# A two-layer streaming encoder step: low halves of the moving operands at multiples of 256 bytes, shared mixer tiles, the residual through another queue

## The chip, the cores and the metric

The kernel runs on one core of one Trainium2 chip. The metric is device time in microseconds of one execution, as the median of several runs; the kernel before took 2676.73 us (three runs, 2674.0 to 2679.26). Profiles come from one further execution of the same program.

## The reference

One inference step for two request groups that share weights: 256 frames of a new stream and 32 next frames of a running one, 288 columns together. Layer 0 is a mixer of retention and gated linear attention (GLA) heads, then a convolutional feed-forward network (FFN); layer 1 is chunked band attention, then an FFN. All is float32, with a model width of 2048.

```
def trunk(x, pos, ret_in, gla_in, k_in, v_in, conv_in, p):
    for l in range(DEPTH):
        h = rmsnorm(x, p['norm_mix_g'][l])
        if l % 2 == 0:
            mix, s_r, s_g = ab_mixer(h, pos, ...)
        else:
            mix, nk, nv = c_mixer(h, ...)
        x = x + mix
        h = rmsnorm(x, p['norm_ffn_g'][l])
        f, buf = conv_ffn(h, ...)
        x = x + f
    y = rmsnorm(x, p['norm_final_g'])

def conv_ffn(h, conv_buf, w_up, conv_w, conv_b, w_down):
    up = jnp.einsum('btd,df->btf', h, w_up)
    g, u = jnp.split(up, 2, axis=-1)
    ...
    act = jax.nn.silu(gc) * u
    return jnp.einsum('btf,fd->btd', act, w_down), gp[:, -(CONV_W - 1):]
```

The outputs are the 288 frames, the new retention and GLA states, the new attention rows and the last rows of the convolutions.

## The kernel before

Activations lie transposed in SBUF: 128 features on the partitions, the 288 frames along them. Every weight matrix is cut into tiles of 128 by 128, and one `project` (L65) makes 128 output features: for each of 16 (or 22) input tiles k it adds products into one PSUM tile of 288 columns, called acc.

A float32 product is made of three faster ones. `weights` (L54) loads a chunk of eight weight tiles (512 KB, through SP's queue, into one of four buffers w), rounds it on ACT into a high part wh (L61, type fp32r) and takes the rest on DVE as a low part wl (L62), three buffers each. The activations are split in the same way, on ACT and DVE, into a high and a low tile. `passes` (L81) then issues three matmuls:

```
        nc.tensor.matmul(ps, lhsT=h, rhs=xh, start=first, stop=False)
        nc.tensor.matmul(ps, lhsT=h, rhs=xl, start=False, stop=False)
        nc.tensor.matmul(ps, lhsT=l, rhs=xh, start=False, stop=last)
```

They are L83, L84 and L85. The weight is the stationary operand, the activation the moving one: 288 columns, 1152 bytes on each partition. L83 and L85 stream the high tile, L84 the low one. The moving operands are named x0 to x15 (the normalised input of a projection; a profile's row says x), and b (16 pairs in one tile: the outputs of the mixers, the input of the output projections and of the FFN's down projection, whose 6 further pairs are b16 to b21 in a pool of the FFN). In each of them the low half stands right behind the high half of the same k.

The stages in order: the first products (L87), where the input x_first comes in ten pieces, each with the residual, two weight columns and a small part of a third for one or two k, and is split as it arrives; the GLA heads and retention heads (`ab_mixer`, L467), whose small full-precision matmuls stand between the projections; the output projection (`out_proj`, L277), which adds each result to the residual x (DVE, L284), squares and splits it for the next norm (ACT L170, DVE L171); the FFN (L288); the attention heads; a second output projection; the second FFN, with the final norm.

The residual x of the first layer is overwritten by squares during the mixer, so it is read again from memory before the output projection (L220, four DMAs of four k each on SP). Its SBUF room is that of the mixer's pool, so the reload waits until the mixer's last users of that room are done, among them the DMAs that write the retention states out (L808).

A tile framework orders the instructions of each engine when the program is built, and gives each a wait for what it needs. An engine and a DMA queue work in order: what stands behind a waiting instruction waits too. SP issues weights and little else; POOL issues the small loads and the outputs and does small copies.

Of the kernel before, what the change touches and what calls it, by code (L numbers as in the profile page):

```python
# [5 lines left out]
F32 = mybir.dt.float32  # L6
F32R = mybir.dt.float32r
# [5 lines left out]
P = 128  # L13
D = 2048
KD = D // P
TP = 256
TS = 32
T = TP + TS
FF = 5632
NF = FF // P  # L20
HALF = NF // 2
# [4 lines left out]
RANK = 16  # L26
# [5 lines left out]
GRP = P // TS  # L32
# [5 lines left out]
class Trunk:  # L38
# [48 lines left out]
    def first_products(self, src, xw, lo_h):  # L87


        nc = self.nc  # L90
        ps = [self.acc_ps.tile([P, 512], F32, name="acc", tag="acc")[:, :T] for _ in range(N_FIRST + 1)]
        cuts = (0, 1, 2, 3, 4, 6, 8, 10, 12, 14, 16)

        for _ in range(8):
            nc.tensor.matmul(self.mm()[:, :P], lhsT=self.ones, rhs=self.ones, start=True, stop=True)
        for c, (i, j) in enumerate(zip(cuts, cuts[1:])):
            n = j - i
            nc.sync.dma_start(xw[:, i:j, :], src[:, i:j, :])
            w = xw[:, i:j, T : T + N_FIRST * P].rearrange("p k (o m) -> p k o m", o=N_FIRST)
            wlo = xw[:, i:j, T + N_FIRST * P :]  # L100
            lo = lo_h[:, i:j, :]
            tile = lambda tag: self.wp.tile([P, WCH, P], F32R, name=tag, tag=tag, bufs=3)[
                :, : N_FIRST * n, :
            ].rearrange("p (k o) m -> p k o m", o=N_FIRST)
            h, l = tile("wh"), tile("wl")
            for k in range(i, j):
                self.gain_in(k, 0)
                if k == i:
                    if c:
                        nc.scalar.copy(h, w)  # L110
                    else:
                        nc.vector.tensor_copy(h, w)
                    nc.vector.tensor_tensor(l, w, h.bitcast(F32), op=ALU.subtract)
                    nc.gpsimd.tensor_copy(lo[:, :, :RANK], wlo)
                    nc.gpsimd.tensor_tensor(
                        lo[:, :, RANK : 2 * RANK], wlo, lo[:, :, :RANK].bitcast(F32), op=ALU.subtract
                    )
                first, last = k == 0, k == KD - 1
                at = k - i
                for o in range(N_FIRST):  # L120
                    nc.tensor.matmul(ps[o], lhsT=h[:, at, o, :], rhs=self.xh[k], start=first, stop=False)
                for o in range(N_FIRST):
                    nc.tensor.matmul(ps[o], lhsT=h[:, at, o, :], rhs=self.xl[k], start=False, stop=False)
                for o in range(N_FIRST):
                    nc.tensor.matmul(ps[o], lhsT=l[:, at, o, :], rhs=self.xh[k], start=False, stop=last)
                nc.tensor.matmul(ps[-1], lhsT=lo[:, at, :], rhs=self.xh[k], start=first, stop=False)
                nc.tensor.matmul(ps[-1], lhsT=lo[:, at, :], rhs=self.xl[k], start=False, stop=last)
        return ps
# [67 lines left out]
    def run(self, ctx):  # L196
        nc, a = self.nc, self.a

        ones = self.const("ones", [P, P + 32])
        self.ones, self.eps = ones[:, :P], ones[:, P : P + 1]  # L200
        xs = [self.const(f"x{k}", [P, 2, T], F32R) for k in range(KD)]
        self.xh, self.xl = [[x[:, i, :] for x in xs] for i in range(2)]
        b_all = self.const("b", [P, KD, 2, T], F32R)
        self.bh_all, self.bl_all = b_all[:, :, 0, :], b_all[:, :, 1, :]
        self.bh, self.bl = [[b_all[:, k, i, :] for k in range(KD)] for i in range(2)]
        self.R = self.const("R", [P, T])
        nc.vector.memset(self.ones, 1.0)
        nc.vector.memset(self.eps, EPS)
        self.gains = self.const("gains", [P, 5, KD], F32, a["gains"], nc.scalar)
        self.sq_last = None  # L210
        with self.tc.tile_pool(name="in", bufs=1) as pool:
            sums = self.start(pool)
        with self.tc.tile_pool(name="ab", bufs=1) as pool:
            self.ab_mixer(pool, *sums)
        with self.tc.tile_pool(name="x", bufs=1) as xp:

            x = xp.tile([P, KD * T + 16], F32, name="x", tag="x")[:, : KD * T].rearrange("p (k t) -> p k t", t=T)
            self.x = [x[:, k, :] for k in range(KD)]
            for k in range(0, KD, 4):
                nc.sync.dma_start(x[:, k : k + 4, :], a["xT"][:, k : k + 4, :])  # L220
            self.out_proj(a["w_out_ab"], 1, (WCH, 0))
            with self.tc.tile_pool(name="f0", bufs=2) as pool:
                self.ffn(pool, 0, 2, x)
            with self.tc.tile_pool(name="c", bufs=2) as pool:
                self.chain(
                    self.att_heads(pool), 3,
                    lambda: self.out_start(a["w_out_att"], (0, WCH), 2),
                )
            self.out_proj(a["w_out_att"], 3, (0, WCH))
            with self.tc.tile_pool(name="f1", bufs=2) as pool:  # L230
                self.ffn(pool, 1, 4, x)
# [18 lines left out]
    def start(self, pool):  # L250

        nc, a = self.nc, self.a
        w = a["w_in"]

        nc.scalar.activation(self.R[:, :1], self.ones[:, :1], AF.Abs_reciprocal_sqrt)
        xw = self._one(pool, "xw", [P, KD, T + N_FIRST * P + RANK])
        x_in = xw[:, :, :T]
        self.x = [x_in[:, k, :] for k in range(KD)]


        lo_h = self._one(pool, "lo_h", [P, KD, P], None, F32R)
        nc.gpsimd.memset(lo_h.bitcast(F32)[:, :, 2 * RANK :], 0.0)
        k0, q0, lo_ps = self.first_products(a["x_first"], xw, lo_h)
        self.ident = self.const("ident", [P, P], F32, a["ident"], nc.sync)

        self.w2 = self.const("w2", [P, 512 + 224])[: 2 * RANK + 1, :512]
        nc.sync.dma_start(self.w2, a["w2"])
        v0 = self.input_product(w[VB])
        self.first_squares(x_in)

        self.norm_stat()
        v1 = self.mm()[:, :T]
        second = lambda part: self.project(w[VB + 1], self.xh, self.xl, KD, chunks=(0, WCH), part=part, ps=v1)
        second(0)
        return k0, q0, v0, lo_ps, second
# [11 lines left out]

    def ffn(self, pool, layer, n, x_all):  # L288
        nc, a = self.nc, self.a
        bs = [self._one(pool, f"b{k}", [P, 2, T], None, F32R) for k in range(KD, HALF)]  # L290
        bh, bl = [old + [b[:, i, :] for b in bs] for i, old in ((0, self.bh), (1, self.bl))]
        convp = self._one(pool, "convp", [P, NF, 4], a["convp"][:, layer])
        hist = self._one(pool, "hist", [P, NF, 2], a["hist"][:, layer])
# [6 lines left out]
        for half in range(2):  # L300
            for fl in range(HALF):
                f = half * HALF + fl
# [18 lines left out]
                v = pool.tile([P, T], F32, name="v", tag="v")  # L321
# [22 lines left out]
        cuts = (0, 1, 4, 8, 12, 16)  # L344
# [22 lines left out]
    def head_out(self, pool, o, gates, hd, g):  # L367

        nc = self.nc
        sq = pool.tile([P, TP], F32, name="hsq", tag="hsq", bufs=1)  # L370
        sq2 = pool.tile([P, TP], F32, name="hsq2", tag="hsq2", bufs=1)
        nc.scalar.activation(sq, o[0], AF.Square)
        nc.scalar.activation(sq2, o[1], AF.Square)
        nc.vector.tensor_tensor(sq, sq, sq2, op=ALU.add)
# [92 lines left out]
    def ab_mixer(self, pool, k0, q0, v0, lo_ps, second):  # L467
# [37 lines left out]

        def ret(hd):
            if hd == 0:
                late["cos"], late["sin"] = one("cosR", [P, T], a["cos"]), one("sinR", [P, T], a["sin"])
                for t in late.values():
                    nc.gpsimd.tensor_tensor(t, t, self.R, op=ALU.mult)  # L510
                late["kdec"] = one("kdec", [P, H_RET, 2], a["kdec"])
            aside = {0: gla_sample, H_RET - 1: ret_sample}.get(hd, iter(()))
            yield from self.ret_head(pool, hd, w, late["cos"], late["sin"], late["kdec"], hg, r4, rst, aside)
# [13 lines left out]
    def gla_head(self, pool, hd, w, sums, masks, eyem, hg, s4, sts, first):  # L527
# [11 lines left out]
        v.append(self.parted(pool, v1, "v1", s4["v"][:, 1, hd, :]))  # L539
        gate = lambda i: self.gate(pool, w[GB + 2 * hd + i], i, s4["z"][:, i, hd, :])  # L540
        z = [gate(0)] if first else []
        st = pool.tile([P, 256], F32, name="gst", tag="gst", bufs=GRP)
        nc.gpsimd.dma_start(st, a["state_gla"][hd])
        sts.append(st)

# [161 lines left out]
    def ret_head(self, pool, hd, w, cosR, sinR, kdec, hg, s4, sts, aside):  # L709
        nc, a = self.nc, self.a  # L710
        dec = pool.tile([P, 384], F32, name="dec", tag="dec")
        nc.gpsimd.dma_start(dec, a["dec"][hd])
        st = pool.tile([P, 2, 256], F32, name="rst", tag="rst", bufs=GRP)
        nc.gpsimd.dma_start(st, a["state_ret"][hd])
        sts.append(st.rearrange("p j v -> p (j v)"))

        def rope(base, name):
            z = [self.input_product(w[base + 2 * hd + i]) for i in range(2)]
# [177 lines left out]
    def att_sample(self, pool, g, kept, v4, bd):  # L896
# [13 lines left out]
        vt = pool.tile([P, P], F32, name="avt4", tag="avt4")  # L910
        nc.scalar.copy(vt, pv)
        s = pool.tile([P, T], F32, name="as4", tag="as4")
        own = pool.tile([P, GRP, TS], F32, name="own4", tag="own4")
        mx = pool.tile([P, 1], F32, name="mx4", tag="mx4")
        sm = pool.tile([P, 1], F32, name="sm4", tag="sm4")
        nc.vector.tensor_tensor(s, ps, bias, op=ALU.add)
# [20 lines left out]
        for i in range(2):  # L937
            for c, (_, _, vc) in zip(quarter, kept):
                nc.tensor.matmul(
                    po[c], lhsT=pT[:, 1 + i, c], rhs=vc[:, i, :], start=False, stop=i == 1, skip_group_check=True  # L940
                )
        o = pool.tile([P, P], F32, name="ao4", tag="ao4")
        nc.vector.tensor_scalar(o, po, sm, None, op0=ALU.mult)
        yield
        ps = self.mm()[:, :P]
# [139 lines left out]
```

## Time and profile before

| | |
|---|---|
| median of three runs | 2676.73 us (2674.0 to 2679.26) |
| the profiled execution | 2679.3 us, its span 2677.2 us |
| granted TensorE clock, mean | 0.998 |
| DMA | 448.27 MB, mean 167 GB/s |
| HBM | read 434.69 MB, written 10.40 MB |

The span runs from the first to the last instruction; the execution has 2.1 us around it. In a profile PE is the matmul engine and PEld its weight load; L83 is line 83 of the kernel. A group's row has its line, engine, operation, the tiles out<-in, the shape and the count; behind the bar the busy time in us and the mean length of one in ns, and then the idle time before it and who ended it. The rows of a timeline begin with the start and the length in us.

### The profile page before, as it was taken

To read this page: it belongs to the slowest core of one execution; us is meant where nothing else is said; L and a number is where in the kernel's file an instruction comes from. 1 tells how busy PE (TensorE), PEld (TensorE's weight loads), DVE (VectorE), ACT (ScalarE), POOL (GpSimd) and SP (SyncE) were. 2 spreads that over 40 slices of the span, in tenths; PEclk is the share of its full clock that TensorE was granted. 3 is DMA by queue.
4 is the path that set the end of the run, shared out by engine and by line. 5 is a ranking of instruction groups with operands and counts; after the bars stand their busy time and mean duration, and the time that the engine had idled before them with its cause. 6 is when DMAs were issued, how large, how long until landed. Compare 5 with 4: busy or idle time off the path is not lost. (4 is left out here: it accounts for less than half of the span.)

```text
span 2677.2 us, 48712 instructions
## 1 busy us (share of the span) xinstructions
PE 2661.0 (99%) x20079; PEld 2642.5 (99%) x20079; DVE 1560.8 (58%) x2593; ACT 1126.1 (42%) x1511; POOL 132.8 (5%) x459
## 2 busy tenths in 40 slices
PE   9999999999999999999999999999999999999998
PEld 9999999999999999999999999999999999999998
DVE  8665555566664456665555555556666545666544
ACT  7564445443333333334444443444333333333443
POOL 3000000000000000000021110000000000000000
PEclk9999999999999999999999999999999999999999
DMA  6444445555555555555565565555555555555554
GB/s 230 151 138 156 157 157 193 167 164 166 166 166 164 167 168 167 165 168 160 166 213 179 178 183 166 158 166 165 166 166 166 163 167 168 166 166 166 165 166 131
DMA packets 127227, 448.27 MB, mean 167 GB/s; under 512 B 16059, under 2 KB 16379, under 8 KB 127004
## 3 DMA queue, kind: packets, MB, share of 16 engines
q1 hardware_dynamic: 119852, 426.83, 51.5%
q0 software_dynamic: 7008, 18.29, 2.2%
q8 instruction: 157, 2.57, 0.4%
q14 instruction: 66, 0.54, 0.1%
q10 hardware_dynamic: 144, 0.04, 0.0%
HBM read 434.69 MB, written 10.40 MB: 166 GB/s over the span
## 5 line engine op out<-in xcount | busy, mean ns | idle before, releaser
L61 ACT CAST wh<-w 128x1024 fp32r<-128x1024 f32 (+1 forms) x812 | 839.2, 1034 | 1461.0 <-PE acc L84 1210.8
L62 DVE TENSOR_TENSOR wl<-w,wh 128x1024 fp32r<-128x1024 f32 (+1 forms) x812 | 976.4, 1203 | 738.4 <-ACT wh L61 737.4
L83 PE MATMUL acc<-x,wh 128*128 128x288 f32 x4432 | 1314.6, 297 | 0.0
L84 PE MATMUL acc<-x,wh 128*128 128x288 f32 x4432 | 1311.8, 296 | 0.0
L85 PE MATMUL acc<-x,wl 128*128 128x288 f32 x4432 | 1308.4, 295 | 0.0
L85 PEld LDWEIGHTS acc<-x,wl 128*128 128x128 f32 x4432 | 839.5, 189 | 0.3
L83 PEld LDWEIGHTS acc<-x,wh 128*128 128x128 f32 x4432 | 833.0, 188 | 1.6 <-issue 1.1
L84 PEld LDWEIGHTS acc<-x,wh 128*128 128x128 f32 x4432 | 833.3, 188 | 0.3
L83 PE MATMUL acc<-b,wh 128*128 128x288 f32 x1920 | 567.4, 296 | 0.5 <-ACT wh L61 0.5
L85 PE MATMUL acc<-b,wl 128*128 128x288 f32 x1920 | 566.2, 295 | 0.7 <-DVE wl L62 0.7
L84 PE MATMUL acc<-b,wh 128*128 128x288 f32 x1920 | 566.9, 295 | 0.0
L85 PEld LDWEIGHTS acc<-b,wl 128*128 128x128 f32 x1920 | 363.2, 189 | 1.2 <-DVE wl L62 1.0
L83 PEld LDWEIGHTS acc<-b,wh 128*128 128x128 f32 x1920 | 360.6, 188 | 1.3 <-ACT wh L61 1.1
L84 PEld LDWEIGHTS acc<-b,wh 128*128 128x128 f32 x1920 | 360.8, 188 | 0.1
L316 DVE SCALAR_TENSOR_TENSOR gc<-gp,convp,gc 128x290 f32<-128x290 f32 x176 | 91.2, 518 | 3.1
L322 DVE TENSOR_TENSOR v<-acc,R 128x288 f32<-128x288 f32 x88 | 40.3, 458 | 88.6 <-PE acc L85 88.6
L307 DVE TENSOR_TENSOR gp<-acc,R 128x256 f32<-128x256 f32 x88 | 37.4, 425 | 90.3 <-PE acc L85 90.1
L309 POOL COPY conv_out<-gp 128x2 f32<-128x2 f32 x88 | 16.4, 187 | 1309.3 <-DVE gp L307 1309.3
L147 ACT CAST b<-v 128x288 fp32r<-128x288 f32 x88 | 38.2, 434 | 16.1 <-DVE v L324 16.1
L323 DVE TENSOR_TENSOR v<-v,sg 128x256 f32<-128x256 f32 x88 | 37.4, 426 | 10.6 <-DVE v L322 1.8
L314 DVE TENSOR_SCALAR gc<-gp,convp 128x290 f32<-128x290 f32 x88 | 38.0, 431 | 9.4
L332 DVE TENSOR_TENSOR x<-x,acc 128x288 f32<-128x288 f32 x64 | 29.1, 454 | 19.2 <-PE acc L85 19.2
(301 smaller groups left out, 1140.1 us busy)
## 6 DMA issues: line engine op xcount, KB each, us to landing
w<-in_w_ffn_up SPq DMA_DIRECT2D x352, 512.0 KB, 3.7
w<-in_w_ffn_down SPq DMA_DIRECT2D x128, 512.0 KB, 3.7
w<-in_w_in SPq DMA_DIRECT2D x108, 512.0 KB, 3.8
w<-in_w_qkv SPq DMA_DIRECT2D x96, 512.0 KB, 3.8
w<-in_w_ffn_down SPq DMA_DIRECT2D x64, 384.0 KB, 3.2
w<-in_w_out_ab SPq DMA_DIRECT2D x32, 512.0 KB, 3.9
w<-in_w_out_att SPq DMA_DIRECT2D x32, 512.0 KB, 3.7
xw<-in_x_first SPq DMA_DIRECT2D x6, 560.0 KB, 7.9
```

Source lines behind the costliest of these rows:

```text
L61: nc.scalar.copy(h, w)
L62: nc.vector.tensor_tensor(l, w, h.bitcast(F32), op=ALU.subtract)
L83: nc.tensor.matmul(ps, lhsT=h, rhs=xh, start=first, stop=False)
L84: nc.tensor.matmul(ps, lhsT=h, rhs=xl, start=False, stop=False)
L85: nc.tensor.matmul(ps, lhsT=l, rhs=xh, start=False, stop=last)
L147: self.nc.scalar.copy(h, v)
L307: nc.vector.tensor_tensor(gp[:, 2 : TP + 2], g[:, :TP], self.R[:, :TP], op=ALU.mult)
L314: nc.vector.tensor_scalar(gc, gp[:, 0:W], cw[:, 0:1], cw[:, 3:4], op0=ALU.mult, op1=ALU.add)
L316: nc.vector.scalar_tensor_tensor(gc, gp[:, w : w + W], cw[:, w : w + 1], gc, op0=ALU.mult, op1=ALU.add)
L322: nc.vector.tensor_tensor(v, u, self.R, op=ALU.mult)
L323: nc.vector.tensor_tensor(v[:, :TP], v[:, :TP], s[:, :TP], op=ALU.mult)
L332: nc.vector.tensor_tensor(self.x[m], self.x[m], ps, op=ALU.add)
```

## The change

It has six parts. The first changes addresses, the others make room for it or move transfers.

1. x0 to x15, b and b16 to b21 get slots of 320 columns (1280 bytes) for each half in place of 288 (1152 bytes). The number of columns used stays 288.
2. The pad behind w2 shrinks from 224 to 32 columns.
3. The reload of the residual goes from SP's queue to POOL's, in eight DMAs of two k in place of four of four.
4. The GLA and retention states share one set of four tiles of 512 columns (st) where there were four of 256 (gst) and four of 512 (rst). Two GLA heads share a tile.
5. cos and sin take the two tiles of the softplus (sp); the second square of `head_out` takes a tile of the normed output (on); own4 and ao4 of the attention have one buffer in place of two.
6. The input pieces of the first products are single k up to k = 7 in place of k = 3.

The addresses in the built program, by their rest over 256 bytes:

| operand | before | after |
|---|---|---|
| high halves of x0 to x15, b, b16 to b21 | 0 | 0 |
| low halves of the same | 128 | 0 |
| weights w, wh, wl (each tile 512 bytes) | 64 | 64 |

```
+TB = 320
-        cuts = (0, 1, 2, 3, 4, 6, 8, 10, 12, 14, 16)
+        cuts = (0, 1, 2, 3, 4, 5, 6, 7, 8, 10, 12, 14, 16)
-        xs = [self.const(f"x{k}", [P, 2, T], F32R) for k in range(KD)]
+        xs = [self.const(f"x{k}", [P, 2, TB], F32R)[:, :, :T] for k in range(KD)]
-        b_all = self.const("b", [P, KD, 2, T], F32R)
+        b_all = self.const("b", [P, KD, 2, TB], F32R)[:, :, :, :T]
-            for k in range(0, KD, 4):
-                nc.sync.dma_start(x[:, k : k + 4, :], a["xT"][:, k : k + 4, :])
+            for k in range(0, KD, 2):
+                nc.gpsimd.dma_start(x[:, k : k + 2, :], a["xT"][:, k : k + 2, :])
-        self.w2 = self.const("w2", [P, 512 + 224])[: 2 * RANK + 1, :512]
+        self.w2 = self.const("w2", [P, 512 + 32])[: 2 * RANK + 1, :512]
-        bs = [self._one(pool, f"b{k}", [P, 2, T], None, F32R) for k in range(KD, HALF)]
+        bs = [self._one(pool, f"b{k}", [P, 2, TB], None, F32R)[:, :, :T] for k in range(KD, HALF)]
-        sq2 = pool.tile([P, TP], F32, name="hsq2", tag="hsq2", bufs=1)
+        sq2 = pool.tile([P, TP], F32, name="on", tag="on", bufs=2)
-                late["cos"], late["sin"] = one("cosR", [P, T], a["cos"]), one("sinR", [P, T], a["sin"])
-                for t in late.values():
+                late["cos"], late["sin"] = [pool.tile([P, T], F32, name="sp", tag="sp", bufs=2) for _ in range(2)]
+                for x, t in late.items():
+                    nc.gpsimd.dma_start(t, a[x])
                     nc.gpsimd.tensor_tensor(t, t, self.R, op=ALU.mult)
-        st = pool.tile([P, 256], F32, name="gst", tag="gst", bufs=GRP)
-        nc.gpsimd.dma_start(st, a["state_gla"][hd])
-        sts.append(st)
+        st = pool.tile([P, 512], F32, name="st", tag="st", bufs=GRP) if hd % 2 == 0 else None
+        sts += [st[:, :256], st[:, 256:]] if hd % 2 == 0 else []
+        nc.gpsimd.dma_start(sts[hd], a["state_gla"][hd])
-        st = pool.tile([P, 2, 256], F32, name="rst", tag="rst", bufs=GRP)
-        nc.gpsimd.dma_start(st, a["state_ret"][hd])
-        sts.append(st.rearrange("p j v -> p (j v)"))
+        st = pool.tile([P, 512], F32, name="st", tag="st", bufs=GRP)
+        nc.gpsimd.dma_start(st.rearrange("p (j v) -> p j v", j=2), a["state_ret"][hd])
+        sts.append(st)
-        own = pool.tile([P, GRP, TS], F32, name="own4", tag="own4")
+        own = pool.tile([P, GRP, TS], F32, name="own4", tag="own4", bufs=1)
-        o = pool.tile([P, P], F32, name="ao4", tag="ao4")
+        o = pool.tile([P, P], F32, name="ao4", tag="ao4", bufs=1)
```

From the diff's first line on, lines of the changed kernel stand one or two further down: the three passes are L84, L85 and L86 there.

SP's queue from the last weights of the mixer to the first of the FFN, before (w is a chunk of weights, in_ names its source, x the residual):

```order
L60 DMA w<-in_w_in 128x1024 x108
L60 DMA w<-in_w_out_ab 128x1024 x10
L220 DMA x<-in_xT 128x1152 x4
L60 DMA w<-in_w_out_ab 128x1024 x22
L60 DMA w<-in_w_ffn_up 128x1024 x88
```

and POOL's queue after the change, from the last outputs of the retention heads (so and st are state tiles, dec a decay mask) to the first loads of the FFN:

```order
L714 DMA dec<-in_dec 128x384
L766 DMA out_ret_out<-so 128x512 x2
L810 DMA out_ret_out<-st 128x512 x4
L221 DMA x<-in_xT 128x576 x8
L526 DMA convp<-in_convp 128x176
L526 DMA hist<-in_hist 128x88
L298 MEMSET gp_6193 128x2
```

The reload has left the place between the tenth and the eleventh chunk of output weights on SP, and stands behind the four outputs of the retention states on POOL, ahead of the FFN's constants.

ACT in the first products, k = 3 to k = 9, before (L170 rounds the high half of x, L110 that of the two weight columns that came with it; x_74 is x3, x_80 is x9):

```order
L170 ACTIVATE x_74<-xw,gains 128x288
L110 CAST wh<-xw 128x256
L170 ACTIVATE x_75<-xw,gains 128x288
L110 CAST wh<-xw 128x512
L170 ACTIVATE x_76<-xw,gains 128x288
L170 ACTIVATE x_77<-xw,gains 128x288
L110 CAST wh<-xw 128x512
L170 ACTIVATE x_78<-xw,gains 128x288
L170 ACTIVATE x_79<-xw,gains 128x288
L110 CAST wh<-xw 128x512
L170 ACTIVATE x_80<-xw,gains 128x288
```

and after:

```order
L171 ACTIVATE x_74<-xw,gains 128x288
L111 CAST wh<-xw 128x256
L171 ACTIVATE x_75<-xw,gains 128x288
L111 CAST wh<-xw 128x256
L171 ACTIVATE x_76<-xw,gains 128x288
L111 CAST wh<-xw 128x256
L171 ACTIVATE x_77<-xw,gains 128x288
L111 CAST wh<-xw 128x256
L171 ACTIVATE x_78<-xw,gains 128x288
L111 CAST wh<-xw 128x256
L171 ACTIVATE x_79<-xw,gains 128x288
L111 CAST wh<-xw 128x512
```

Two casts of 512 columns have become four of 256, each ahead of the next k's rounding.

## The prediction

> **What bounds the kernel now.** I read the page first, then busy time in stretches, then the timeline of PE at two places.
>
> ```profile
> PE   2661.0 (99%) x20079; PEld 2642.5 (99%) x20079; DVE 1560.8 (58%) x2593; ACT 1126.1 (42%) x1511; POOL 132.8 (5%) x459
> PEclk9999999999999999999999999999999999999999
> L84 PE MATMUL acc<-x,wh 128*128 128x288 f32 x4432 | 1311.8, 296 | 0.0
> L85 PE MATMUL acc<-x,wl 128*128 128x288 f32 x4432 | 1308.4, 295 | 0.0
> L84 PE MATMUL acc<-b,wh 128*128 128x288 f32 x1920 | 566.9, 295 | 0.0
> ```
>
> PE is busy for 2661 of 2677 us at an undisturbed clock, and no matmul group of the three passes waits. L83 (high x high), L84 (high weight, **low** moving operand) and L85 (low weight, high moving operand) run 4432 + 1920 = 6352 times each on the groups x and b, so some 19,060 matmuls of 288 columns make up the time. DVE and ACT have half of it free. The 295 ns of one matmul is its whole pipelined life; what counts is the step from one start to the next, which stretches give.
>
> ```profile
> 460.00:536.00 76.00, 76.00 (x577) 76.00 (x576) 45.08 (x61) 36.21 (x51) 0.00 (x0) 1.00 0.56 176
> 600.00:760.00 160.00, 160.00 (x1209) 160.00 (x1208) 100.40 (x163) 62.27 (x75) 6.25 (x38) 1.00 0.52 166
> ```
>
> The second and third columns are the stretch and PE's busy time, with the matmuls that touch it (one that reaches in counts, so I add its 0.295 us). In the first output projection the step is 76.295/577 = 132.2 ns, in the first FFN 160.295/1209 = 132.6 ns. At 19,060 steps that is some 2525 us: the kernel's time is this step, and 0.1 ns of it is 1.9 us. What is left, some 150 us, is full-precision matmuls of the mixers, the start and the end.
>
> **The change part by part.**
>
> *Moving operands.* In the built program every high operand starts at a multiple of 256 bytes already, and every low one 1152 bytes behind it, so 128 bytes off. After the change both start at multiples. Weights stay 64 bytes off a multiple. So L83's and L85's operands keep their kind of place and only L84's changes it: a third of the matmuls. No instruction is added or removed. What is it worth? The two stretches again, step by step:
>
> ```profile
> 999.93 0.30 PE L83 MATMUL acc<-x,wh 128*128 128x288 f32 x1
> 1000.06 0.29 PE L84 MATMUL acc<-x,wh 128*128 128x288 f32 x1
> 1000.20 0.29 PE L85 MATMUL acc<-x,wl 128*128 128x288 f32 x1
> 1000.33 0.29 PE L83 MATMUL acc<-x,wh 128*128 128x288 f32 x1
> 1000.46 0.29 PE L84 MATMUL acc<-x,wh 128*128 128x288 f32 x1
> 1000.59 0.29 PE L85 MATMUL acc<-x,wl 128*128 128x288 f32 x1
> 1000.72 0.29 PE L83 MATMUL acc<-x,wh 128*128 128x288 f32 x1
> 1000.85 0.30 PE L84 MATMUL acc<-x,wh 128*128 128x288 f32 x1
> 1000.99 0.30 PE L85 MATMUL acc<-x,wl 128*128 128x288 f32 x1
> 1001.12 0.30 PE L83 MATMUL acc<-x,wh 128*128 128x288 f32 x1
> ```
>
> ```profile
> 499.94 0.30 PE L83 MATMUL acc<-b,wh 128*128 128x288 f32 x1
> 500.07 0.29 PE L84 MATMUL acc<-b,wh 128*128 128x288 f32 x1
> 500.20 0.30 PE L85 MATMUL acc<-b,wl 128*128 128x288 f32 x1
> 500.34 0.29 PE L83 MATMUL acc<-b,wh 128*128 128x288 f32 x1
> 500.47 0.29 PE L84 MATMUL acc<-b,wh 128*128 128x288 f32 x1
> 500.60 0.29 PE L85 MATMUL acc<-b,wl 128*128 128x288 f32 x1
> 500.73 0.30 PE L83 MATMUL acc<-b,wh 128*128 128x288 f32 x1
> ```
>
> In the FFN the step that ends an L84 is 0.14, 0.13, 0.14 us and all six others 0.13: nine steps take 1.19 us. That repeats every nine matmuls in each FFN stretch I read. In the output projection six steps take 0.79 us, a different rhythm, and there the long step belongs to L85. By the unrounded start times the steps that end L83, L84, L85 average 131.9, 133.6, 132.2 ns in the FFN stretch and 132.0, 131.3, 133.3 in the other; single steps run from 130 to 136. Over all matmuls of the groups above, steps over 160 ns left out, the three are 131.95, 133.32 and 132.37, mean 132.55.
>
> So PE falls into one of two rhythms, in both FFNs into the longer one, in which the pass with the shifted operand is the slow one. The three passes differ in nothing but that shift, since both weight tiles have the same offset; something about it breaks the symmetry. **The value I take**: L84's step falls to the mean of the two aligned passes, (131.95 + 132.37)/2 = 132.16. That is (133.32 - 132.16) x 6352 = **-7.4 us**. The bounds: with three equal passes a new rhythm may settle anywhere between the shortest and the longest of what is seen: all at 130.0 gives -2.55 x 19,060 = -48.6 us, all at L84's 133.6 gives +1.05 x 19,060 = +20 us.
>
> The output projection's row speaks against the gain, since there the shifted pass is the fastest. So do these:
>
> ```profile
> L853 PE MATMUL mm<-ak,aq 128*128 128x256 f32 x32 | 9.6, 380 | 0.0
> L762 PE MATMUL mm<-vt,kt 128*128 128x256 f32 x32 | 7.6, 379 | 0.0
> ```
>
> Full-precision matmuls of 256 columns take 380 ns with a moving operand 32 or 160 bytes off (ak) and 379 with an aligned one (vt). They stream at half the rate, though. The Trainium skill, "SBUF — State Buffer", Specifications, knows 16-byte lines and nothing coarser on the engine side; 0 and 128 are both multiples of 16, and by that alone the term would be nothing. No run here separates the two.
>
> *The first products.* Pieces 4 to 7 of the first input come one by one.
>
> ```profile
> 8.15 0.54 ACT L170 ACTIVATE x<-xw,gains 128x288 fp32r<-128x288 f32 x1 [0.63 <-DMA xw<-in_x_first]
> 8.60 0.60 ACT L110 CAST wh<-xw 128x512 fp32r<-128x512 f32 x1
> 9.25 0.53 PE L121 MATMUL acc<-x,wh 128*128 128x288 f32 x2 [0.55 <-ACT wh L110]
> ```
>
> ACT waits 0.63 us for the first piece of two, and PE 0.55 us behind it. A single piece comes sooner and its cast is shorter, which can take away the whole 0.55 us; but two casts of 512 columns become four of 256, and if each of the two more costs ACT half of the 0.60, that gives it back. Between -0.6 and +0.6 us; I take **-0.4**, near the wait that the row shows, since ACT stood idle there.
>
> *The residual.* Four DMAs leave SP, eight go to the end of POOL's queue.
>
> ```profile
> 448.38 1.85 SPq L220 DMA_DIRECT2D x<-in_xT  x4
> 448.95 0.54 POOL L524 DMA_DIRECT2D convp<-in_convp  x1 [4.41 <-DMA out_ret_out<-rst]
> 452.80 0.82 DVE L284 TENSOR_TENSOR x<-x,acc 128x288 f32<-128x288 f32 x2 [3.84 <-DMA x<-in_xT]
> 453.42 0.54 ACT L170 ACTIVATE x<-x,gains 128x288 fp32r<-128x288 f32 x1 [5.72 <-DVE x L284]
> 455.72 1.98 ACT L61 CAST wh<-w 128x1024 fp32r<-128x1024 f32 x2
> 456.80 0.40 PE L83 MATMUL acc<-b,wh 128*128 128x288 f32 x1 [0.50 <-ACT wh L61]
> 458.06 0.40 PE L85 MATMUL acc<-b,wl 128*128 128x288 f32 x1 [0.73 <-DVE wl L62]
> ```
>
> On SP the reload waited until 448.38 us with weights behind it. But what PE waits for at 456 to 458 us (0.50 + 0.73 us, 1.2 in all) is casts that stand behind the residual on ACT and DVE. The residual cannot start before the states are written out (448.4 on SP, 448.95 for convp on POOL), whichever queue it has, and the rows on ACT and DVE are in the same order after. Landing decides:
>
> ```profile
> x<-in_xT SPq DMA_DIRECT2D x4, 576.0 KB, 6.8
> rst<-in_state_ret POOLq DMA_DIRECT2D x4, 256.0 KB, 3.6
> ak<-in_cache_k POOLq DMA_DIRECT2D x16, 128.0 KB, 5.1
> ```
>
> A 288 KB piece from POOL should land 3.6 to 5.1 us after its issue at about 448.5, so at 452.1 to 453.6; before it was 452.8. I take **0**, between -1.2 (the wait is gone) and +0.8 (it lands 0.8 us later). Behind the eight issues (8 x 0.54 = 4.3 us) stand convp, hist and the gp memsets, not needed before the FFN at 538 us.
>
> *Sharing.* cos and sin now wait for the softplus tiles, two of four retention states for the GLA states to be written out, own4, ao4 and hsq2 for their predecessors. Each wait is for work done tens of us earlier than its consumer, on engines that the page shows half idle, and PE's rows in the mixers wait for none of them: 0, at worst the 1.2 us that late casts cost above; nothing excludes a gain of the same size where the scheduler shifts a row.
>
> **Sum**: -7.4 - 0.4 + 0 = -7.8 us. The profiled execution took 2679.3 us (span 2677.2), 2.6 above the median of 2676.73, so 2671.5 against its own time, and for the median 2676.7 - 7.8 = **2669 us**.
>
> **The rivals.**
>
> *No change* (2676): the rhythm, not the shift, sets the step. For it: two rhythms with the same addresses, one with L84 fastest; equal aligned and shifted full-precision rows. Against: L84 is slowest wherever the nine-step rhythm runs. Between -4 and +4 us.
>
> *Slower* (2696): three equal passes lock into a longer step at PE, in both FFNs and projections. The aligned passes also show long steps (L85 133.3 in the projection); if all settle at 133.6 ns, it costs 20 us. It decides as soon as the mean passes 132.55 + 0.28 = 132.83 ns (0.28 x 19,060 = 5.4 us, 0.2%, about what a measurement of this kernel can tell from no change).
>
> *A shorter rhythm* (2653): all settle at L84's best, 131.3: -1.25 x 19,060 = -24 us; at the extreme 130.0, 2628.
>
> *The whole overhead goes* (2467): if the step beyond pure streaming were a price of shifted operands, it would vanish.
>
> ```profile
> 426.93 1.89 PE L762 MATMUL mm<-vt,kt 128*128 128x256 f32 x8
> ```
>
> Eight such records take 1.89 us; less the 379 ns of the last, seven steps of 216 ns. They stream at half rate, so 288 columns at full rate would take an estimated 216 x 288/512 = 121.5 ns, 11 less than now: 11 x 19,060 = 210 us. Against it: the aligned passes of today step at 132 as well. The Trainium skill, "TensorE: Matmul & The Clock Gate", Back-to-back issue gap, has N/2.4 + 2.5 ns when warm, an estimate of 122.5 here; the trace's 132.6 disagrees, and by that rule the time would be some 190 us less.
>
> **How the numbers follow.** Forecast 0.36, no change 0.27, slower 0.19, a shorter rhythm 0.14, the whole overhead 0.04. Of the forecast's own spread (-4 to -11 us) 0.03 lies within 0.2%. So faster 0.33 + 0.14 + 0.04 = 0.51, same 0.30, slower 0.19. The range takes in both bounds of the unknown step, 2628 to 2697.
>
> **What would show it.** Right: L85 of the new kernel (the low operand's pass) steps like its neighbours, and stretches in the FFNs fall from 132.6 to about 132.2 ns; only there is the time. ACT's wait at 453 us stays near 5.7 us and PE's at 456 near 1.2. Wrong: a step outside 131.3 to 133.3, a rhythm unchanged at 1.19 us per nine, or new waits of PE in the mixers before 440 us.

## The result, and the profile after

| | before | after |
|---|---|---|
| median of the runs side by side | 2676.8 us (2674.0 to 2679.26) | 2697.91 us (2695.91 to 2698.18) |
| ratio | | 1.0078, interval 1.006 to 1.0095 |
| span of the profiled execution | 2677.2 us | 2696.4 us |
| mean step between starts of the three passes | 132.55 ns | 133.32 ns |

The change makes the kernel 21 us slower. The forecast was 2669; the time lies 0.9 us above the range's upper end. The steps in this text are differences of unrounded start times of neighbouring matmuls of the three passes, those over 160 ns left out (some 18,900 per kernel). One of the ten executions of the kernel before with its weights moved ran at a granted clock of 0.555 and took 4356 us; it is left out of the times below. Lines of the changed kernel are L84 (high weight, high operand), L85 (high weight, low operand), L86 (low weight, high operand).

The page of after first, in the parts that the prediction showed of before:

```profile
PE 2678.4 (99%) x20079; PEld 2660.1 (99%) x20079; DVE 1560.4 (58%) x2595; ACT 1126.4 (42%) x1513; POOL 138.3 (5%) x471
L85 PE MATMUL acc<-x,wh 128*128 128x288 f32 x4432 | 1310.6, 296 | 0.0
L86 PE MATMUL acc<-x,wl 128*128 128x288 f32 x4432 | 1311.7, 296 | 0.0
L84 PE MATMUL acc<-b,wh 128*128 128x288 f32 x1920 | 569.4, 297 | 2.9 <-ACT wh L62 2.9
x<-in_xT POOLq DMA_DIRECT2D x8, 288.0 KB, 7.6
```

The same number of matmuls keeps PE busy 17.4 us longer, at almost unchanged length of one. A busy time that grows with no wait in the row is a longer step. Only the last two rows show something else: a wait of 2.9 us at ACT's cast, and a slow landing of the residual. Busy time in the same two stretches (columns as in the prediction):

```profile
460.00:536.00 76.00, 73.90 (x533) 73.56 (x534) 44.64 (x62) 34.27 (x49) 0.47 (x5) 0.96 0.54 170
600.00:760.00 160.00, 160.00 (x1202) 160.00 (x1201) 100.03 (x163) 62.43 (x75) 6.36 (x39) 1.00 0.53 165
```

In the FFN stretch 1202 matmuls stand where 1209 stood: 160.295/1202 = 133.36 ns in place of 132.6. In the output projection PE has idle time and a granted clock of 0.96. The timeline of PE in the FFN:

```profile
999.88 0.29 PE L84 MATMUL acc<-x,wh 128*128 128x288 f32 x1
1000.01 0.30 PE L85 MATMUL acc<-x,wh 128*128 128x288 f32 x1
1000.15 0.29 PE L86 MATMUL acc<-x,wl 128*128 128x288 f32 x1
1000.28 0.30 PE L84 MATMUL acc<-x,wh 128*128 128x288 f32 x1
1000.41 0.29 PE L85 MATMUL acc<-x,wh 128*128 128x288 f32 x1
1000.54 0.30 PE L86 MATMUL acc<-x,wl 128*128 128x288 f32 x1
1000.68 0.29 PE L84 MATMUL acc<-x,wh 128*128 128x288 f32 x1
1000.81 0.30 PE L85 MATMUL acc<-x,wh 128*128 128x288 f32 x1
```

Six steps take 0.80 us (999.88 to 1000.68). The unrounded steps alternate between 130 and 136 or 137 ns from one matmul to the next, whichever pass it is, and all three passes average 133.3. The rhythm of nine is gone, and no pass is faster than another. This holds in every stage, so it is worth (133.32 - 132.55) x 19,060 = 14.7 us.

The other loss, in the timeline around the reload:

```profile
451.44 4.24 POOL L221 DMA_DIRECT2D x<-in_xT  x8 [4.53 <-DMA out_ret_out<-st]
457.70 0.82 DVE L285 TENSOR_TENSOR x<-x,acc 128x288 f32<-128x288 f32 x2 [6.34 <-DMA x<-in_xT]
458.31 0.54 ACT L171 ACTIVATE x<-x,gains 128x288 fp32r<-128x288 f32 x1 [8.22 <-DMA x<-in_xT]
460.60 2.92 ACT L62 CAST wh<-w 128x1024 fp32r<-128x1024 f32 x3
461.69 0.61 PE L84 MATMUL acc<-b,wh 128*128 128x288 f32 x1 [2.94 <-ACT wh L62]
462.94 0.61 PE L86 MATMUL acc<-b,wl 128*128 128x288 f32 x1 [0.41 <-DVE wl L63]
463.59 0.45 PE L85 MATMUL acc<-b,wh 128*128 128x288 f32 x1
463.83 0.45 PE L86 MATMUL acc<-b,wl 128*128 128x288 f32 x1
```

DVE waits 6.34 us for the residual (before 3.84) and ACT 8.22 (before 5.72). The casts of the next weights stand behind them, so PE waits 2.94 + 0.41 us where it waited 1.23. Its next matmuls start 0.24 us apart in place of 0.13. Busy time of PE in stretches shows why:

```profile
460.00:468.00 8.00, 5.90 (x23) 0.58 0.67 212
468.00:536.00 68.00, 68.00 (x512) 1.00 0.53 165
```

The granted clock was 0.58 over these 8 us, then 1.00 again. Some 19 matmuls ran at half speed, 19 x 0.107 = 2 us. Adding up what each step between 458.4 and 468.2 us has over 0.133 us gives 6.5 us. Before, two gaps of 0.8 and 1.0 us between starts stood at this place, the clock stayed at 1.00, and the same sum over that place is 1.8 us. So the changed kernel loses 4.7 us more here. The Trainium skill, "TensorE: Matmul & The Clock Gate", Part 1, has half clock after an idle window of about 3.4 us; here a shorter gap, 3.24 us between two starts, was enough.

### The profile page after: what moved, and what is told of

Same layout as the page of the kernel before. It is cut to its first block, busy times and chain, and to the rows that moved or that the text cites. A ratio compares the mean times of both kernels' runs of the same rounds, so it can differ in the third digit from the quotient of the medians.

```text
span 2696.4 us, 48741 instructions
## 1 busy us (share of the span) xinstructions
PE 2678.4 (99%) x20079; PEld 2660.1 (99%) x20079; DVE 1560.4 (58%) x2595; ACT 1126.4 (42%) x1513; POOL 138.3 (5%) x471
## 4 chain that ended last, share of the span: by engine, by line
PE 96%; issue 3%; ACT 0%; DMA 0%; DVE 0%; POOL 0%; DVEq 0%; POOLq 0%; ACTq 0%
PE acc L86 30%; PE acc L84 30%; PE acc L85 30%; PE mm L577 0%; PE mm L891 0%; PE mm L855 0%; DMA x<-in_xT 0%; PE mm L764 0%; PE acc L122 0%; PE acc L124 0%; PE acc L126 0%; PE mm L643 0%; PE mm L395 0%; DMA out_ret_out<-st 0%; DVE y L347 0%
## 5 line engine op out<-in xcount | busy, mean ns | idle before, releaser
L84 PE MATMUL acc<-x,wh 128*128 128x288 f32 x4432 | 1315.6, 297 | 0.0
L86 PE MATMUL acc<-x,wl 128*128 128x288 f32 x4432 | 1311.7, 296 | 0.0
L85 PE MATMUL acc<-x,wh 128*128 128x288 f32 x4432 | 1310.6, 296 | 0.0
L84 PEld LDWEIGHTS acc<-x,wh 128*128 128x128 f32 x4432 | 832.2, 188 | 1.6 <-issue 1.1
L85 PEld LDWEIGHTS acc<-x,wh 128*128 128x128 f32 x4432 | 832.1, 188 | 0.3
L86 PEld LDWEIGHTS acc<-x,wl 128*128 128x128 f32 x4432 | 832.0, 188 | 0.3
L84 PE MATMUL acc<-b,wh 128*128 128x288 f32 x1920 | 569.4, 297 | 2.9 <-ACT wh L62 2.9
L86 PE MATMUL acc<-b,wl 128*128 128x288 f32 x1920 | 568.5, 296 | 0.4 <-DVE wl L63 0.4
L85 PE MATMUL acc<-b,wh 128*128 128x288 f32 x1920 | 568.3, 296 | 0.0
L84 PEld LDWEIGHTS acc<-b,wh 128*128 128x128 f32 x1920 | 361.5, 188 | 3.8 <-ACT wh L62 3.5
L86 PEld LDWEIGHTS acc<-b,wl 128*128 128x128 f32 x1920 | 361.4, 188 | 1.0 <-DVE wl L63 0.8
L85 PEld LDWEIGHTS acc<-b,wh 128*128 128x128 f32 x1920 | 361.5, 188 | 0.1
L324 DVE TENSOR_TENSOR v<-v,sg 128x256 f32<-128x256 f32 x88 | 37.5, 426 | 9.2
```

The lines of the kernel that those rows point to most:

```text
L324: nc.vector.tensor_tensor(v[:, :TP], v[:, :TP], s[:, :TP], op=ALU.mult)
```

## The experiments

Two theories stood first: the step follows where the low half lies (15 us), and the reload costs the rest (5 us). All runs but those marked "of before" start from the changed kernel with its reload put back on SP, the first run below.

### Which part costs what

**Reload back on SP.**

```
-            for k in range(0, KD, 2):
-                nc.gpsimd.dma_start(x[:, k : k + 2, :], a["xT"][:, k : k + 2, :])
+            for k in range(0, KD, 4):
+                nc.sync.dma_start(x[:, k : k + 4, :], a["xT"][:, k : k + 4, :])
```

> The changed kernel with one thing undone: the residual is read again through SP's queue, in four DMAs of four k. Theory (the changed kernel's 21 us are two separate losses: about 15 from the steps, about 5 from the reload): 2693 us, 4 to 5 under the changed kernel's 2697.9; the DVE wait for x is near 3.8 us and ACT's near 5.7 as in the kernel before, and the three passes keep their mean step of 133.33 ns. Rival (the reload's longer wait comes from the other edits, such as the shared tiles, and not from the queue and the pieces): 2697 to 2698, waits of 6.3 and 8.2 us as in the changed kernel. Second rival (the step follows what is done at the reload): steps near 132.5, under 2685.

Measured: 2692.98 us, ratio to before 1.0051 (1.0036 to 1.0066), step 133.32 ns. So the reload is 4.9 us of the 21 by the two times (7 by the two ratios, as the kernel before took 2678.9 us beside this run and 2676.8 beside the changed kernel), and it has nothing to do with the step.

**Low half back behind the high half**, by these slots (the same form for b and b16 to b21):

```
+TB, XH, XL = 320, 0, 288
-        xs = [self.const(f"x{k}", [P, 2, TB], F32R)[:, :, :T] for k in range(KD)]
-        self.xh, self.xl = [[x[:, i, :] for x in xs] for i in range(2)]
+        xs = [self.const(f"x{k}", [P, 2 * TB], F32R) for k in range(KD)]
+        self.xh, self.xl = [[x[:, i : i + T] for x in xs] for i in (XH, XL)]
```

> As the run before, with the low half put back right behind the high half (at 1152 bytes of the same 2560, so 128 over a multiple of 256); every other address stays. Theory (where the low half lies against the high one sets the step): the mean step falls from 133.33 to about 132.55 ns, 19,060 steps give 15 us, so 2678. Rival (the weights, which moved by 256 bytes against a multiple of 512, or the slots' pitch of 2560, changed the step): steps stay at 133.33, 2693.

Measured: 2677.76 us, ratio 0.9993 (0.9984 to 1.0002), step 132.45 ns. Moving the low half by 128 bytes, with every other address kept, gives back 15.2 us. What is left of the change (shared tiles, finer pieces, the slots' pitch) has no effect that this can show.

**Low half at 128 with a gap** (XL = 352).

> As the run before, but with the low half at 1408 bytes, again 128 over a multiple of 256, with a gap of 256 bytes behind the high half. Theory A (what counts is the low half's start against the high half's, modulo 256): the step is that of the run before, 132.55 ns if that was right, 2678. Theory B (what counts is that the low half begins in the 256 bytes in which the high half ends): 133.33, 2693.

Measured: 2678.42 us, ratio 0.9998 (0.9988 to 1.0007), step 132.56 ns. How near the two halves lie to each other does not count; the place modulo 256 does.

**Both halves at 128** (XH, XL = 32, 352).

> As the first run, with both halves 128 bytes over a multiple of 256 (at 128 and 1408). Theory (three passes that all begin alike settle at one step, 133.33 ns, wherever that beginning is): 2693. Rival 1 (a start at a multiple of 256 is the dear one, 133.33, and a start at 128 the cheap one): all three near 132 or under, 2668 or less. Rival 2 (the change's own idea, that a start at a multiple of 256 is the cheap one): over 133.33, 2700 or more.

Measured: 2668.18 us, ratio 0.9959 (0.9945 to 0.9974), step 132.10 ns. This refutes "three equal passes settle at 133.33": three equal passes can be faster than the mixture. The change had moved the low half from a cheap place to a dear one.

### Place of the operand, or place against the weight

**The weights moved by 128 bytes**, the moving operands left at the dear place. A smaller pad of w2 puts wh and wl 128 bytes lower, and with them the raw weights w, the norm's scratch tiles, the mixer's tiles and the residual; a larger pad of the residual's tile leaves b16 to b21 where they were, as x0 to x15 and b are (`...` stands for the rest of a line):

```
-        self.w2 = self.const("w2", [P, 512 + 32])[: 2 * RANK + 1, :512]
+        self.w2 = self.const("w2", [P, 512 + 0])[: 2 * RANK + 1, :512]
-            x = xp.tile([P, KD * T + 16], F32, name="x", tag="x")...
+            x = xp.tile([P, KD * T + 48], F32, name="x", tag="x")...
```

> As the run with the reload back on SP (both halves at a multiple of 256), with the weights wh and wl 128 bytes lower, at 192 over a multiple of 256 in place of 64; the moving operands stay. Moving start less weight start is then 64 modulo 256, the same as in the run with both halves at 128. Theory (the moving operand's own place decides): step 133.32 ns, 2693 us. Rival (it is the place of moving operand against weight, as of two reads that meet in the same memory): the step of the run with both halves at 128, 132.10 ns, 18,921 steps of 1.22 ns less, so 2670.

Measured: 2669.93 us, ratio 0.9962 (0.9949 to 0.9975), step 131.97 ns. My theory fell here: the moving operands had not moved, and 23 us went. What counts is the place of the moving operand against that of the weight. (In all runs the tiles named above move together with wh and wl. A matmul reads only wh or wl of them, so I take the difference to these; no run moved wh and wl alone.)

**Both halves at 64** (XH, XL = 16, 336) and **both at 192** (XH, XL = 32, 352 and the pad of ones 16 wider, those of w2 16 narrower and x 16 wider).

> Both halves at 64 over a multiple of 256 (at 64 and 1344), the weights at 64 as well. Theory A (any start off the multiple of 256 is cheap): 132.1 ns, 2668. Theory B (only a half that ends at a multiple of 256, as one that starts at 128 does, is cheap): 133.3, 2693. Theory C (it falls evenly with the start): 132.7, 2681.

> Both halves at 192 over a multiple of 256, so that each touches six stretches of 256 bytes in place of five. Theory A (any start off the multiple is cheap): 132.1 ns, 2668. Theory B (only a half that ends at a multiple of 256 is cheap): 133.3, 2693. Theory D (the step follows the count of stretches touched): over 133.3, 2700 or more.

Measured: 2661.81 us, ratio 0.9937 (0.9923 to 0.9952), step 131.67 ns; and 2693.24 us, ratio 1.0055 (1.004 to 1.007), step 133.33 ns. None of the theories that knew the moving operand alone gives both. By the difference to the weight these are 0 and 128.

**The weights at 0**, with both halves at 0 (pads of w2 and x: 16 and 32); **both halves at 96** (XH, XL = 24, 344), the weights at 64.

> As the run with the reload back on SP, but the weights 64 bytes lower, at a multiple of 256, as both halves are. Theory (moving start less weight start, modulo 256, sets the step: 0 gave 131.67 ns, 64 about 132.0, 128 and 192 133.33): the difference is 0, so 131.67 ns and 2662 us. Rival (the two places act each by itself, and 0 is a bad place of the moving operand): at most what the weights' move by 128 gained, 132.0 to 133.3, 2670 to 2693.

> Both halves at 96 over a multiple of 256, the weights at 64: a difference of 32, between the two cheap ones. Theory (a smooth dependence on the difference): between 131.67 and 132.1 ns, 2662 to 2670. Rival (what counts is whether the difference is a multiple of 64, or there is a minimum between): under 131.5, below 2658, or over 132.5, above 2677.

Measured: 2661.66 us, ratio 0.9937 (0.9922 to 0.9952), step 131.66 ns: a difference of 0 again, at another place, with the same step. And 2693.32 us, ratio 1.0055 (1.004 to 1.007), step 133.34 ns: 32 is dear, so the dependence is not smooth. That left open whether a start off a multiple of 64 is dear by itself. Three runs for it: **everything at 96** (pads of w2 and x: 40 and 8), **halves at 64 with weights at 32** (pads 24 and 24), **both halves at 80** (XH, XL = 20, 340).

> Both halves at 96 over a multiple of 256 as in the run of 2693.3 us, and the weights 32 bytes higher, at 96 as well: the difference is 0. Theory (only the difference of moving start and weight start counts): 131.67 ns, 2662 us. Rival (a moving operand that does not start at a multiple of 64 is dear by itself): 133.3, 2693.

> Both halves at 64 as in the run of 2661.8 us, the weights 32 bytes lower, at 32 over a multiple of 256: the difference is 32. Theory (only the difference counts, and 32 is a dear one): 133.33 ns, 2693 us. Rival (the place modulo 64 of the moving operand made 96 dear): 131.7 to 132, 2662 to 2670.

> Both halves at 80 over a multiple of 256, the weights at 64: a difference of 16. Theory (only differences that are 0 or 64 are cheap): 133.3 ns, 2693. Rival (the cheap place is a narrow stretch around 0): 131.7 to 132, 2662 to 2670, or less.

Measured: 2661.69 us, ratio 0.9943 (0.993 to 0.9957), step 131.67 ns; 2693.16 us, ratio 1.0061 (1.0047 to 1.0075), step 133.34 ns; 2660.37 us, ratio 0.994 (0.9927 to 0.9954), step 131.63 ns. A difference of 0 is cheap at 96 too, and one of 32 is dear at 64 too. The difference decides, and 16 is as cheap as 0; my narrower theory for the third run (only 0 and 64 are cheap) was wrong.

The stretch of the FFN, PE alone, shows it without any arithmetic on records: the count in the same 160 us. First the run with the weights at 0, then that with halves at 64 and weights at 32, then that with both at 128:

```profile
600.00:760.00 160.00, 160.00 (x1217) 1.00 0.51 166
```

```profile
600.00:760.00 160.00, 160.00 (x1202) 1.00 0.50 165
```

```profile
600.00:760.00 160.00, 160.00 (x1212) 1.00 0.53 167
```

All runs in one table; starts are given modulo 256 bytes:

| high, low, weight | high - weight, low - weight | step, ns | in 160 us | us |
|---|---|---|---|---|
| 0, 0, 0 | 0, 0 | 131.66 | 1217 | 2661.7 |
| 64, 64, 64 | 0, 0 | 131.67 | 1217 | 2661.8 |
| 96, 96, 96 | 0, 0 | 131.67 | 1217 | 2661.7 |
| 80, 80, 64 | 16, 16 | 131.63 | 1218 | 2660.4 |
| 96, 96, 64 | 32, 32 | 133.34 | 1202 | 2693.3 |
| 64, 64, 32 | 32, 32 | 133.34 | 1202 | 2693.2 |
| 128, 128, 64 | 64, 64 | 132.10 | 1212 | 2668.2 |
| 0, 0, 192 | 64, 64 | 131.97 | 1213 | 2669.9 |
| 192, 192, 64 | 128, 128 | 133.33 | 1202 | 2693.2 |
| 0, 0, 64 (after, reload on SP) | 192, 192 | 133.32 | 1202 | 2693.0 |
| 0, 128, 64 (before) | 192, 64 | 132.55 | 1209 | 2676.8 |

The mean of a kernel can hide levels. In the output projections and the FFNs, 57 stretches of 30 us in each of the traces, the mean step of a stretch is within 0.06 ns of one of only four values: 131.67, 132.22, 132.59 or 133.33 ns. At a difference of 0 or 16 it is always the first, at 32, 128 or 192 always the last. At 64 it is the first or the second, so 132.10 and 131.97 are mixtures. The kernels with 192 and 64 mixed stand at the second or third, the one with 0 and 128 mixed (below) always at the second. As a rule a whole stage keeps to one value. The first and the second FFN of the run with the weights moved by 128 bytes (1213 and 1217 matmuls):

```profile
600.00:760.00 160.00, 160.00 (x1213) 1.00 0.51 166
1900.00:2060.00 160.00, 160.00 (x1217) 1.00 0.51 167
```

Why a stage takes the one or the other with the same addresses is not known.

### The kernel before with the weights alone moved

**Of before**: pad of w2 208 in place of 224, that of x 32 in place of 16; slots of 1152 bytes as they were.

> The kernel before, slots of 1152 bytes as they were, with the weights alone 64 bytes lower, at a multiple of 256. The high half then stands at a difference of 0 to the weight, the low half at 128. Theory (difference of the places): two passes of 131.67 and one of 133.33, mean 132.2 against 132.5, so 2670 to 2672; no wider slot is needed for it. Rival (the weights' place counts only where both halves lie alike): 2676 to 2678.

Measured: 2673.97 us, ratio 0.9983 (0.9973 to 0.9993), step 132.29 ns. Faster, as the difference says, by 5 us of the run of before beside it; the absolute time came out 2 us above the expected span.

### The reload

**Of before, reload on POOL** in eight DMAs of two k, and **of before, eight DMAs on SP**:

```
-            for k in range(0, KD, 4):
-                nc.sync.dma_start(x[:, k : k + 4, :], a["xT"][:, k : k + 4, :])
+            for k in range(0, KD, 2):
+                nc.gpsimd.dma_start(x[:, k : k + 2, :], a["xT"][:, k : k + 2, :])
```

> The kernel before with only the reload changed: eight DMAs of two k on POOL's queue. Theory (the reload by itself costs the 5 us by which the changed kernel and its run with the reload back differ): 2682, steps unchanged at 132.55 ns, DVE's wait for x about 6.3 us and ACT's about 8.2, then some matmuls of 240 ns. Rival (it costs only together with the shared tiles or the queue's other loads of the changed kernel): 2677 to 2678, waits of 3.8 and 5.7 us.

> The kernel before with the reload in eight DMAs of two k, still on SP's queue. Theory (POOL's queue is what costs the 5 us: it is released later and issues each DMA in 0.54 us): 2677, DVE's wait for x near 3.8 us, ACT's near 5.7. Rival (the small pieces cost): 2681 to 2682, waits of 6 and 8 us.

Measured: 2682.47 us, ratio 1.0016 (1.0006 to 1.0026), with waits of 6.2 and 8.1 us; and 2675.9 us, ratio 0.9989 (0.9979 to 0.9999). On POOL's queue the reload alone costs 4.9 us by the medians (1.6 to 7 by the ratio's interval), on SP's the same pieces cost nothing. The timelines, POOL's first:

```profile
448.30 4.24 POOL L220 DMA_DIRECT2D x<-in_xT  x8 [4.26 <-DMA out_ret_out<-rst]
454.68 0.82 DVE L284 TENSOR_TENSOR x<-x,acc 128x288 f32<-128x288 f32 x2 [6.23 <-DMA x<-in_xT]
```

```profile
448.50 3.87 SPq L220 DMA_DIRECT2D x<-in_xT  x8
451.52 0.82 DVE L284 TENSOR_TENSOR x<-x,acc 128x288 f32<-128x288 f32 x2 [5.35 <-DMA x<-in_xT]
```

Both queues are released at the same time (448.3 and 448.5; SP with pieces of four k 448.38). The first piece is usable 6.4 us after its issue on POOL and 3.0 on SP (4.4 with pieces of four k, before). Neither the release nor the issue (4.24 against 3.87 us for eight) makes that difference; the way from issue to landing does. The records of single packets in the two traces split the 3.4 us. The reload's first packet starts 2.46 us after the issue on POOL and 0.97 on SP (1.5 us). Its first 288 KB are in after 4.58 and 2.38 us (0.7 us more): on POOL 0.68 MB of weights moved in that time, on SP none, since there the weights stand behind the reload. DVE starts 1.80 and 0.64 us after that (1.2 us more). So by leaving SP's queue the reload also lost its place ahead of the weights. That the weights cost it the 0.7 us is likely but not shown, and why its first packet starts later and DVE follows later is open.

### Both cures together

**Halves and weights at 0, reload on SP in eight DMAs of two k.**

> Both halves and the weights at a multiple of 256 (difference 0), the reload on SP's queue in eight DMAs of two k. Theory (the two gains add up: 17 us of the steps, 1 of the smaller pieces): 2660 to 2661, against 2661.7 with four pieces. Rival (the small pieces gain nothing, as PE waits for something else there): 2662.

Measured: 2660.36 us, ratio to before 0.994 (0.9926 to 0.9953), step 131.67 ns. It beats both kernels: 17 us under the kernel before, 37.5 under the changed one. The run with both halves at 80 comes to the same time with the reload in four pieces, so what the small pieces save (1.3 us against the same addresses with four) is at the edge of what these runs can tell.

## Why the prediction was wrong, point by point

- *PE's step is the kernel's time, 0.1 ns of it 1.9 us*: right. From the lowest to the highest step of the table (131.63 to 133.34) that gives 1.71 x 19,060 = 32.6 us; measured were 32.9 (2693.3 - 2660.4).
- *"L84's step falls to the mean of the two aligned passes"*, -7.4 us: **the step that failed**. It took alignment for the cheap place, and it read the three averages of a rhythm as the prices of the three operands. In place of it the runs show that the difference between moving start and weight start counts: with all three passes alike they step at 133.32 ns for 192, where the high half stood, and at about 132.0 for 64, where the low half stood. The change put the low half at 192 too. In a pipeline locked to a rhythm, the long step need not be that of the pass that causes it: before, the longest step in the FFNs began with the low operand, which was the cheap one. Only the mean over the rhythm is a price, and even means need not add up. Two thirds of 133.32 and one third of 132.0 are 132.9, but the kernel before stepped at 132.55 (0.3 ns, some 6 us); for the kernel before with its weights at 0 the same sum gives 132.2, and 132.29 was measured. What sets the step of a mixture stays open.
- *"Weights stay 64 bytes off a multiple"* stood in the prediction as a remark. It was half of the cause, and no term of the sum used it. The rows of ak and vt (380 and 379 ns), which the prediction counted against the gain, could not tell: in the built program ak and its weight aq start both at 32 or both at 160, vt and its weight kt both at 0, so each of these differences is 0. All starts here are multiples of 16, so the 16-byte lines of the Trainium skill, "SBUF — State Buffer", Specifications, which the prediction weighed, would make these kernels alike; the runs differ by 33 us.
- *The rival "Slower"* (three equal passes settle at a longer step, +20 us): the outcome and nearly its size (+14.7 of the 21). Its reason was wrong, since three equal passes settle anywhere from 131.63 to 133.34 with the difference. Of the other two rivals, neither 131.3 nor 121.5 ns was seen over a kernel; the lowest is 131.63.
- *Residual, 0 us, between -1.2 and +0.8*: wrong in size, +4.9. The term took 3.6 to 5.1 us from issue to landing for a piece on POOL, from rows of single loads at other places; it was 6.4 in the run on POOL of before (and 6.3 after). What followed was left out: a stall of 3 us at PE, after which its clock was halved for some 7 us (0.51 granted from 461 to 468 us).
- *First products, -0.4 us*: within its bounds. The main loop's first L84 starts at 23.14 us after against L83's 23.38 before; two profiles with the same code there (after, and with the reload back) differ by 0.5 us, so no more can be said.
- *Sharing, 0 us*: as predicted; the run with the low half behind the high one has all of it and stands at 0.9993 of before.

## What to carry to other kernels

Where matmuls run back to back, print the start addresses of weights and moving operands modulo 256 together: here their difference, not the alignment of either, was worth 33 us of 2660, and changing two pads was enough to set it. Do not read the price of one operand off one phase of a locked rhythm; change all phases alike and compare means. A load that others wait for in order should not be moved to another queue on the ground that both queues are released together: compare issue to landing on that queue, at that place, and look at what the transfer then runs beside.

## What the runs showed that was not expected

- The step of a 288-column fp32r matmul takes values between 131.63 and 133.34 ns with the difference of the two operands' starts modulo 256 bytes: 0 and 16 cheap, 64 between, 32, 128 and 192 dear, and within a projection or FFN at one of four levels. Slots at 256 over a multiple of 512 (the high halves after, 133.31 and 133.32 ns) and at 0 (the low halves, 133.34) step alike. That weight load and streaming meet in reading memory would fit, but was not shown; other differences were not tried.
- In seven of the nine kernels with all three passes at one difference of 0, 32, 128 or 192 the times of a kernel lie within 0.9 us (in the other two within 2.3); at 16 they spread by 3.6 us, at 64 and with 192 and 64 mixed by 4 to 9 us (before 2674.0 to 2679.26), with 0 and 128 mixed by 1.2. The kernels with 192 and 64 mixed fall into one rhythm or another at the same differences (1209 or 1212 matmuls in the same 160 us), and so do those at 64 (1212 to 1217).
- After a gap of 3.24 us between two matmuls (3.17 in the run of before with the reload on POOL) the granted clock was halved for some 7 us (0.51 from 461 to 468 us; 0.57 over 4 us there); after one of 1.0 us it was not.
